# The opening of a two-layer encoder step: first loads reordered over two queues, first weights halved and scaled on ScalarE, spills held behind the first query weights

## The chip, the cores and the metric

The kernel runs on one core of a Trainium2 chip. The metric is the device time of one execution in microseconds (us), lower is better. Profiles are taken by the hardware profiler from one execution of the program. Engines are called PE (TensorE, matmul), DVE (VectorE), ACT (ScalarE), POOL (GpSimd) and SP (SyncE, which here only issues DMAs). PEld is the loading of PE's stationary operand, which runs beside its matmuls.

## The reference, cut to what matters

One inference step of a small encoder with two layers of width 1024. It takes a prompt of 1024 new frames and, beside it, 128 frames of eight running streams ("sample"). Both layers have attention and a squared-ReLU MLP; the first has its own queries, keys and values, the second shares one projection of keys and values. What the change touches is the opening of the first layer:

```
def rmsnorm(x, g):
    y = xf * lax.rsqrt(jnp.mean(xf * xf, axis=-1, keepdims=True) + EPS)
    return (y * g).astype(x.dtype)
...
def project_a(x, g_norm, w_qkv, g_q, g_k):
    qkv = rmsnorm(x, g_norm) @ w_qkv
    q, k, v = jnp.split(qkv, [1024, 1280], axis=-1)
    q = rmsnorm(q.reshape(b, t, 16, 64), g_q)
    k = rmsnorm(k.reshape(b, t, 4, 64), g_k)
    return q, k, v
```

After it come, for the prompt, attention over a window of whole chunks with a distance penalty and a learned sink, for the sample the same over a cache; then the output projection, the residual and the MLP. Everything is in float32.

## The kernel before, in words

**Precision.** A float32 operand is written as a sum of two parts, hi (rounded to the type that PE reads) and lo (the rest). A product takes three matmuls: hi by hi, hi by lo, lo by hi (`proj`, L178 to L184; in the profile L182, L183, L184 of a 128-row block k). So each operand of PE is first split, in two instructions: one rounds, one subtracts (`split`, L106 to L115, ACT and DVE as a rule).

**Tiles.** The 1024 prompt rows are eight tiles of 128 rows (t = 0 to 7), the 128 sample rows are a ninth, ST. The normalization is folded: the gain g goes into the rows of the weights, the row's inverse root mean square is applied later.

**Loads.** `load_block` (L122) brings a block of 1024 x 512 weights in four loads of two row blocks (512 KB), on SP's queue, into one of four raw buffers of [128, 2, 512]; `split_g` (L147) scales each row block k by its column of gains `gcol`: the hi part on POOL in this layer (L152; its configuration has the letter g), the lo part on DVE (L155). `prep_gains` (L1128) fills `gcol` before all else: five loads on SP (L1137), one transpose on PE in a PSUM pool of its own (L1139), one copy on DVE (L1140).

**The opening of layer 0** (L1514 on), with functions that are closures of `attention`:
- `X(t)` (L1304) loads a tile of x on SP's queue into one of two buffers "x" (L1313).
- `N(t)` (L1315) turns it: eight 128x128 transposes on PE (L175), two casts hh on ACT (L109) and two subtractions hl on DVE (L115); then the row statistics on ACT (L166) and small steps on DVE and POOL. Tile 0 has the buffers hh, hl (one of each), tile 1 borrows those of the attention's transposed probabilities, ST those of its probabilities p.
- `K1(t)` (L1365) is the projection of keys and values, eight row blocks of three matmuls with the block wkv; those of tiles 0, 1 and ST are woven, row block by row block (L1567). `K2(t)` (L1373) turns and splits the keys, and copies them half to half by two DMAs on SP (L278, L279).
- `Q1(t, 0)` (L1381) is the projection of the first half of the queries with the block wq, again eight row blocks of three; at its end ACT squares and copies the result (L191, L192; one buffer qr), DVE reduces, POOL takes the root (L203), DVE scales (L204). `Q2(t, 0)` (L1387) turns qr on PE (L225) and splits it into one of two buffers qT.
- `spill(t)` (L1339) stores hh and hl of a tile to device memory in four stores of 256 KB on SP (L1343), as the second half of the queries reads them back later (`R`, L1345).
- `sinks`, `load_gvec` load small constants on SP (L590, L1238 to L1247).

After the opening, a loop over steps and groups (`V`, `U`, plan) weaves scores, probabilities, transposes, later projections and the sample's units.

**What sets the order.** The code gives a program order, which is each instruction's priority. A scheduler then fixes the order of every engine's and queue's instructions by a simulated timeline: it picks, of what is ready in the simulation, the first by priority. Buffers of a pool are handed out in the same pass, and every wait is made from the resulting order. `behind(a, b)` (L715) adds an order between two instructions of a queue without a wait. In layer 0 no part has a raised priority, and no order is written out by hand.

Of the kernel before, what the change touches and what calls it, by code (L numbers as in the profile page):

```python
# [8 lines left out]
F32 = mybir.dt.float32  # L9
# [7 lines left out]
P = 128  # L17
D = 1024
KC = D // P
NT = 8  # L20
ST = NT
# [54 lines left out]
class Build:  # L76
# [44 lines left out]

    def load_block(self, dst, w, n0, g, ks=range(0, KC, 2)):  # L122
        nc = self.nc
        wr = w.rearrange("(k p) n -> p k n", p=P)
        for k0 in ks:
            raw = self.raw([P, 2, 512])
            nc.sync.dma_start(raw, wr[:, k0 : k0 + 2, n0 : n0 + 512])
            self.split_g(dst[:, 0, k0 : k0 + 2, :], dst[:, 1, k0 : k0 + 2, :], raw, g, k0)

# [16 lines left out]

    def split_g(self, hi, lo, raw, g, k0):  # L147
        nc = self.nc
        for k in range(raw.shape[1]):
            s = self.gcol[:, g * KC + k0 + k : g * KC + k0 + k + 1]  # L150
            if "g" in self.engs:
                nc.gpsimd.tensor_scalar(hi[:, k], raw[:, k], s, 1.0, ALU.mult, ALU.mult)  # L152
            else:
                nc.scalar.activation(hi[:, k], raw[:, k], AF.Copy, scale=s)
            nc.vector.scalar_tensor_tensor(  # L155
                lo[:, k], raw[:, k], s, hi[:, k].bitcast(F32), ALU.mult, ALU.subtract
            )
# [969 lines left out]

    def prep_gains(self):  # L1128
        nc, I = self.nc, self.ins
        with ExitStack() as st:  # L1130
            self.psum_pools(st, "pg", dict(m=(1, 1)), dict(m="m"))
            tmp = self.pool(st, "tmpg")
            g = tmp.tile([5 * KC, P], F32, tag="g", name="g")
            for i, v in enumerate(
                (I["g_attn"][0], I["g_attn"][1], I["g_mlp"][0], I["g_mlp"][1], I["g_kv"])
            ):
                nc.sync.dma_start(g[i * KC : (i + 1) * KC, :], v.rearrange("(k p) -> k p", p=P))  # L1137
            ps = self.psum("m", [P, 5 * KC], "ps_g")
            nc.tensor.transpose(ps, g, self.ident[0 : 5 * KC, 0 : 5 * KC])  # L1139
            nc.vector.tensor_copy(self.gcol, ps)  # L1140

# [10 lines left out]
    def run(self):  # L1152
# [9 lines left out]
        with ExitStack() as top:  # L1162
# [39 lines left out]

            self.prep_gains()
            flat = lambda a: a.rearrange("b s h d -> (b s) (h d)")
# [53 lines left out]
    def attention(self, layer):  # L1258
# [17 lines left out]
        with ExitStack() as st:  # L1276
# [27 lines left out]
            def X(t):  # L1304
                if A:
                    xr[t] = work.tile([P, D], F32, tag="x", name="x", bufs=2)
                elif t == ST:
                    nb = cfg["bias_bufs"]
                    x = ring.tile([P, G, 256], F32, tag="biasB", name="x", bufs=nb)
                    xr[t] = x.rearrange("p g k -> p (g k)")  # L1310
                else:
                    xr[t] = self.rawp.tile([P, D], F32, tag="raw", name="x")
# [26 lines left out]
            def spill(t):  # L1339
                for z in range(2):  # L1340
                    c = slice(4 * z, 4 * z + 4)
                    for v in range(2):
                        nc.sync.dma_start(self.hTd[t][:, v, c], hts[t][v][z].bitcast(F32))  # L1343

# [172 lines left out]
            wkv = self.wslot()  # L1517
            if A:
                X(0)
                self.load_block(wkv, wkv_src, kv0, gkv, [0])  # L1520
                X(1)
                N(0)
                self.load_block(wkv, wkv_src, kv0, gkv, [2])
                X(ST)
                N(1, "pt")
                self.load_block(wkv, wkv_src, kv0, gkv, [4, 6])
                N(ST, "p")
# [56 lines left out]
            spill(1)  # L1584
            run(Q1(1, 0, "s"))
            K2(1)
            spill(ST)
            run(Q1(ST, 0, "s"))
            K2(ST)
            X(2)  # L1590
            Q2(0, 0)
            N(2)
# [196 lines left out]
```

## Time and profile before

| | |
|---|---|
| median of 3 runs | 2400.1 us |
| lowest and highest | 2393.41 and 2401.02 us |
| the profiled execution's own time | 2396.21 us |
| its span, first to last instruction | 2394.4 us |
| mean granted clock of PE | 0.993 |
| bytes read and written in device memory | 246.47 and 136.14 MB |

The span lies 1.8 us inside the profiled execution's own time. A row of the order of time has the start and duration in us, the engine, the line, the operation, output and input by the program's names, and the count; in brackets the idle time of the engine before it and what ended it. SPq is SP issuing DMAs, not the transfer. A row of grouped instructions has the busy time and the mean ns of one. A row of stages gives the stretch, its length, and for each engine the busy time and count, then the clock that PE was granted (1.00 is full), the busy share of the 16 DMA engines and GB/s.

### The profile page before, as it was taken

The numbers are of one execution on the slowest core, as the hardware profiler recorded it, in microseconds if no ns is written. First come the engines' busy times: TensorE is split into PE (matmuls) and PEld (weight loads), VectorE is DVE, ScalarE is ACT, GpSimd is POOL, SyncE is SP. The second block draws the span as 40 slices with busy tenths as digits, with TensorE's granted clock in tenths as the row PEclk, the third lists the DMA queues.
The fourth block names the chain that finished last, engine by engine and source line by source line (L and its number), as shares of the span: only waits on it lengthen the run. The fifth ranks groups of instructions, "written<-read, shape, count | busy, mean of one in ns | idle before, by whom it ended". The sixth has DMA issues, their size and how long they took to land.

```text
span 2394.4 us, 33443 instructions
## 1 busy us (share of the span) xinstructions
PE 2315.4 (97%) x11621; PEld 1932.2 (81%) x11621; DVE 1629.9 (68%) x3002; ACT 1212.0 (51%) x2415; POOL 542.5 (23%) x836
## 2 busy tenths in 40 slices
PE   7999999899999999999999999998999999999999
PEld 6777877788888878888777788876888888888887
DVE  6787786755655767776577876877655555777674
ACT  3776675555555432332277666665555555323321
POOL 4343332312212100000243444444111211000000
PEclk9998999999999999999999999999999999999999
DMA  7345545344433874342754655555433445734332
GB/s 253 119 132 166 171 155 193 103 150 157 145 129 141 324 245 141 112 141 100 246 155 114 197 163 169 166 167 171 141 133 137 154 141 202 275 138 158 114 115 115
DMA packets 218393, 385.88 MB, mean 161 GB/s; under 512 B 50344, under 2 KB 125040, under 8 KB 211056
## 3 DMA queue, kind: packets, MB, share of 16 engines
q1 hardware_dynamic: 195152, 307.18, 39.0%
q0 software_dynamic: 21776, 71.84, 7.8%
q10 hardware_dynamic: 1296, 4.72, 0.5%
q8 instruction: 92, 1.51, 0.3%
q14 instruction: 77, 0.63, 0.1%
HBM read 246.47 MB, written 136.14 MB: 160 GB/s over the span
## 4 chain that ended last, share of the span: by engine, by line
PE 81%; DVE 7%; DMA 6%; ACT 3%; issue 2%; POOL 1%; SPq 0%; POOLq 0%; ACTq 0%; DVEq 0%
PE ps_x L711 9%; PE ps_x L713 9%; PE ps_x L712 9%; PE ps_y L713 7%; PE ps_y L712 7%; PE ps_y L711 7%; PE ps_mm L182 3%; PE ps_mm L184 3%; PE ps_mm L183 3%; PE ps_tr L289 2%; PE ps_mm L143 2%; PE ps_mm L145 2%; PE ps_mm L144 2%; PE ps_s L713 1%; PE ps_s L712 1%
## 5 line engine op out<-in xcount | busy, mean ns | idle before, releaser
L109 ACT CAST w<-r 128x2048 fp32r<-128x2048 f32 x56 | 107.1, 1913 | 321.6 <-PE ps_y L713 210.6
L711 PE MATMUL ps_x<-w,s 128*128 128x512 f32 x512 | 199.5, 390 | 4.3 <-DVE x L1017 2.2
L713 PE MATMUL ps_x<-w,s 128*128 128x512 f32 x512 | 199.4, 389 | 0.0
L712 PE MATMUL ps_x<-w,s 128*128 128x512 f32 x512 | 199.2, 389 | 0.0
L182 PE MATMUL ps_mm<-w,hh 128*128 128x512 f32 x432 | 174.2, 405 | 9.7 <-DMA hh<-hTd 3.3
L184 PE MATMUL ps_mm<-w,hl 128*128 128x512 f32 x432 | 174.1, 404 | 1.7 <-DMA hl<-hTd 1.6
L183 PE MATMUL ps_mm<-w,hh 128*128 128x512 f32 x432 | 172.5, 400 | 1.6 <-DVE w L155 1.6
L109 ACT CAST s<-s 128x2048 fp32r<-128x2048 f32 x56 | 107.2, 1914 | 121.3 <-DMA s<-hd 112.2
L115 DVE TENSOR_TENSOR w<-r,w 128x2048 fp32r<-128x2048 f32 x56 | 128.2, 2289 | 51.0 <-ACT w L109 51.0
L711 PE MATMUL ps_x<-sx,w 128*128 128x512 f32 (+1 forms) x408 | 157.9, 387 | 3.8 <-ACT hc L830 2.9
L1017 DVE TENSOR_TENSOR x<-ps_y,x 128x512 f32<-128x512 f32 x136 | 92.3, 687 | 99.8 <-PE ps_y L713 99.8
L713 PE MATMUL ps_x<-sx,w 128*128 128x512 f32 (+1 forms) x408 | 154.1, 378 | 0.0
L712 PE MATMUL ps_x<-sx,w 128*128 128x512 f32 (+1 forms) x408 | 154.1, 378 | 0.0
L109 ACT CAST w<-ru 128x512 fp32r<-128x512 f32 (+1 forms) x160 | 110.0, 708 | 85.4 <-PE ps_y L712 32.0
L713 PE MATMUL ps_y<-w,s 128*128 128x512 f32 x384 | 149.5, 389 | 0.0
L711 PE MATMUL ps_y<-w,s 128*128 128x512 f32 x384 | 149.4, 389 | 0.0
L712 PE MATMUL ps_y<-w,s 128*128 128x512 f32 x384 | 149.4, 389 | 0.0
L115 DVE TENSOR_TENSOR s<-s 128x2048 fp32r<-128x2048 f32 x56 | 128.0, 2286 | 30.4 <-ACT s L109 30.3
L115 DVE TENSOR_TENSOR ptl<-ps_tr,pth 128x512 fp32r<-128x512 f32 x180 | 122.6, 685 | 24.2 <-ACT pth L109 18.6
L115 DVE TENSOR_TENSOR w<-ru,w 128x512 fp32r<-128x512 f32 (+1 forms) x160 | 126.4, 792 | 11.2 <-ACT w L109 11.2
L115 DVE TENSOR_TENSOR wq<-ru,wq 128x1024 fp32r<-128x1024 f32 x32 | 39.7, 1240 | 132.2 <-ACT wq L109 132.2
L109 ACT CAST pth<-ps_tr 128x512 fp32r<-128x512 f32 x180 | 104.8, 595 | 45.6 <-PE ps_tr L289 33.2
(279 smaller groups left out, 6570.6 us busy)
## 6 DMA issues: line engine op xcount, KB each, us to landing
s<-hd SPq DMA_DIRECT2D x56, 1024.0 KB, 4.7
ru<-in_w_up SPq DMA_DIRECT2D x64, 512.0 KB, 3.8
r<-in_w_down SPq DMA_DIRECT2D x32, 1024.0 KB, 5.8
hd<-hc POOLq DMA_DIRECT2D x128, 256.0 KB, 2.7
hd<-hs POOLq DMA_DIRECT2D x96, 256.0 KB, 2.5
x<-xd SPq DMA_DIRECT2D x41, 512.0 KB, 4.5
o<-oTd SPq DMA_DIRECT2D x52, 256.0 KB, 3.9
hTd<-hh SPq DMA_DIRECT2D x36, 256.0 KB, 3.9
```

The source lines that it names most:

```text
L109: a = nc.scalar.copy(hi, src)
L115: return a, e.tensor_tensor(lo, src, hi.bitcast(F32), ALU.subtract)
L143: nc.tensor.matmul(ps, oh[:, k, :], w[:, 0, k, nn], start=(k == 0), stop=False)
L144: nc.tensor.matmul(ps, oh[:, k, :], w[:, 1, k, nn], start=False, stop=False)
L145: nc.tensor.matmul(ps, ol[:, k, :], w[:, 0, k, nn], start=False, stop=(k == 3))
L182: nc.tensor.matmul(ps, a, w[:, 0, k, :], start=(k == 0), stop=False)
L183: nc.tensor.matmul(ps, a, w[:, 1, k, :], start=False, stop=False)
L184: nc.tensor.matmul(ps, b, w[:, 0, k, :], start=False, stop=(k == KC - 1))
L711: a = mm(ps, ah, bh, start=first, stop=False, skip_group_check=True)
L712: mm(ps, ah, bl, start=False, stop=False, skip_group_check=True)
L713: return a, mm(ps, al, bh, start=False, stop=last, skip_group_check=True)
L1017: tt(xs[t][:, N[n]], ps, xs[t][:, N[n]], ALU.add)
```

## The change

It touches the opening of layer 0 in six ways.

1. The gains are loaded by `load_gains` on ACT's queue in three loads instead of five on SP's, into a buffer of the attention's pool, and turned by `turn_gains` in the attention's PSUM bank, after `N(0)`.
2. In program order the loads are x(0), the first two row blocks of wkv, x(1), the next two, x(ST), the last four. `N(0)` stands ahead of the first weights.
3. The wkv loads come in pieces of one row block (256 KB), and their hi part is scaled on ACT (`first=True`). Later blocks keep 512 KB and POOL.
4. x(ST) lies in one of the two qT buffers instead of one of the two x buffers.
5. Each weight load of `load_block` is kept as `self.gate`; the spills of tiles 0, 1 and ST are ordered on their queue behind the last of them, which is then the last piece of the first query weights wq.
6. `Q2(0, 0)` stands before `K2(1)` instead of after the load of x(2).

```diff
-    def load_block(self, dst, w, n0, g, ks=range(0, KC, 2)):
+    def load_block(self, dst, w, n0, g, ks=range(0, KC, 2), first=False):
...
             raw = self.raw([P, 2, 512])
-            nc.sync.dma_start(raw, wr[:, k0 : k0 + 2, n0 : n0 + 512])
-            self.split_g(dst[:, 0, k0 : k0 + 2, :], dst[:, 1, k0 : k0 + 2, :], raw, g, k0)
+            step = 1 if first else 2
+            for k in range(0, 2, step):
+                self.gate = nc.sync.dma_start(
+                    raw[:, k : k + step], wr[:, k0 + k : k0 + k + step, n0 : n0 + 512]
+                )
+            self.split_g(dst[:, 0, k0 : k0 + 2, :], dst[:, 1, k0 : k0 + 2, :], raw, g, k0, first)
...
-            if "g" in self.engs:
+            if "g" in self.engs and not first:
                 nc.gpsimd.tensor_scalar(hi[:, k], raw[:, k], s, 1.0, ALU.mult, ALU.mult)
             else:
                 nc.scalar.activation(hi[:, k], raw[:, k], AF.Copy, scale=s)
...
-    def prep_gains(self):
+    def load_gains(self, pool):
         nc, I = self.nc, self.ins
...
+        g = pool.tile([5 * KC, P], F32, tag="pvt", name="g", bufs=1)
+        n = 2 * KC
+        for i, v in enumerate((I["g_attn"], I["g_mlp"])):
+            nc.scalar.dma_start(g[i * n : (i + 1) * n, :], v.rearrange("l (k p) -> (l k) p", p=P))
+        nc.scalar.dma_start(g[2 * n :, :], I["g_kv"].rearrange("(k p) -> k p", p=P))
+        return g
+
+    def turn_gains(self, g):
+        nc = self.nc
+        ps = self.psum("m", [P, 5 * KC], "ps_g")
+        nc.tensor.transpose(ps, g, self.ident[0 : 5 * KC, 0 : 5 * KC])
+        nc.vector.tensor_copy(self.gcol, ps)
...
-            self.prep_gains()
...
-                if A:
+                if A and t == ST:
+                    xr[t] = apool.tile([P, D], F32, tag="qT", name="x", bufs=2)
+                elif A:
...
-                        nc.sync.dma_start(self.hTd[t][:, v, c], hts[t][v][z].bitcast(F32))
+                        d = nc.sync.dma_start(self.hTd[t][:, v, c], hts[t][v][z].bitcast(F32))
+                        if t in (0, 1, ST):
+                            self.behind(self.gate, d)
...
             if A:
+                g = self.load_gains(apool)
                 X(0)
-                self.load_block(wkv, wkv_src, kv0, gkv, [0])
+                N(0)
+                self.turn_gains(g)
+                self.load_block(wkv, wkv_src, kv0, gkv, [0], True)
                 X(1)
-                N(0)
-                self.load_block(wkv, wkv_src, kv0, gkv, [2])
+                self.load_block(wkv, wkv_src, kv0, gkv, [2], True)
                 X(ST)
                 N(1, "pt")
-                self.load_block(wkv, wkv_src, kv0, gkv, [4, 6])
+                self.load_block(wkv, wkv_src, kv0, gkv, [4, 6], True)
                 N(ST, "p")
...
             run(Q1(1, 0, "s"))
+            Q2(0, 0)
             K2(1)
             spill(ST)
             run(Q1(ST, 0, "s"))
             K2(ST)
             X(2)
-            Q2(0, 0)
             N(2)
```

More of the change, by code (lines that the diff above doesn't have):

```diff
@@ L145, in wo_proj, with split_g @@
             nc.tensor.matmul(ps, ol[:, k, :], w[:, 0, k, nn], start=False, stop=(k == 3))
-    def split_g(self, hi, lo, raw, g, k0):
+    def split_g(self, hi, lo, raw, g, k0, first=False):
         nc = self.nc
@@ L1126, in prep_bias @@
             nc.sync.dma_start(self.biasSd[0:KV].rearrange("j p c -> p j c"), big)
-    def prep_gains(self):
+    def load_gains(self, pool):
         nc, I = self.nc, self.ins
[L1130 to L1140, printed above, removed]
+        g = pool.tile([5 * KC, P], F32, tag="pvt", name="g", bufs=1)
[9 more added lines that the diff above has]
+        nc.vector.tensor_copy(self.gcol, ps)
     def token_scales(self, t, need_r):
```

## The prediction

> **What bounds the kernel now.** I read the page first (how busy TensorE, PE, is), then the busy time by stages, then the order of time of single engines where PE is not full.
>
> ```profile
> span 2394.4 us, 33443 instructions
> PE 2315.4 (97%) x11621; PEld 1932.2 (81%) x11621; DVE 1629.9 (68%) x3002; ACT 1212.0 (51%) x2415; POOL 542.5 (23%) x836
> ```
>
> PE is the bound: only 2394.4 - 2315.4 = 79 us of the span are without a matmul. The change can win idle PE time or PE time at a low clock, and only at the start. The stages (stretch, its length, busy us and count of PE, PEld, DVE, ACT, POOL; then granted clock, DMA share, GB/s):
>
> ```profile
> core 0: us, PE busy (x) PEld busy (x) DVE busy (x) ACT busy (x) POOL busy (x), PEclk, DMA share, GB/s
> 4.03:6.54 2.51, 0.30 (x1) 0.18 (x1) 0.20 (x1) 0.08 (x1) 0.00 (x0) 1.00 0.90 323
> 6.54:10.20 3.66, 3.63 (x16) 3.27 (x16) 1.67 (x6) 3.58 (x7) 0.60 (x2) 1.00 1.00 340
> 10.20:13.20 3.00, 0.02 (x1) 0.00 (x0) 2.64 (x5) 0.64 (x2) 3.00 (x5) 1.00 0.94 358
> 15.50:20.65 5.15, 5.14 (x12) 4.08 (x13) 5.11 (x11) 1.15 (x2) 2.71 (x3) 0.50 0.48 168
> 20.80:52.06 31.26, 31.26 (x146) 25.84 (x145) 18.64 (x37) 7.29 (x18) 14.89 (x18) 1.00 0.75 272
> 52.06:56.00 3.94, 2.14 (x19) 1.90 (x18) 3.01 (x7) 3.90 (x8) 2.15 (x2) 1.00 0.76 225
> 56.00:80.00 24.00, 21.48 (x104) 17.20 (x104) 17.34 (x65) 14.64 (x47) 6.75 (x13) 0.93 0.51 167
> ```
>
> PE in order of time (start, duration, and the idle time before it with its releaser):
>
> ```profile
> 4.06 0.30 PE L1139 MATMUL ps_g<-identr,g 40*128 40x40 f32 x1 [4.06 <-DMA g<-in_g_kv]
> 6.57 3.65 PE L175 MATMUL ps_n<-identr,x 128*128 128x128 f32 x16 [2.21 <-DMA x<-in_x_prompt]
> 13.20 0.73 PE L182 MATMUL ps_mm<-w,hh 128*128 128x512 f32 x2 [2.99 <-POOL w L152]
> 15.51 0.80 PE L183 MATMUL ps_mm<-w,hh 128*128 128x512 f32 x1 [1.57 <-DVE w L155]
> 23.65 1.03 PE L175 MATMUL ps_n<-identr,x 128*128 128x128 f32 x8
> ```
>
> The first projection matmul comes at 13.20, after PE has waited for x, then for weights scaled by POOL and DVE. At clock 0.50 twelve matmuls take 5.15 us, 0.43 each. From 20.80 PE is full for 31.26 us: 132 matmuls of 512 columns and 14 small ones (0.13 each by the 23.65 row), so (31.26 - 1.8)/132 = 0.22 each. All 144 matmuls of K1 and the first Q1 thus cost 32 us at full clock, whatever the loads do. The question is when PE reaches that steady stream. My **mark** is 20.80: 15 projection matmuls and 16 transposes done, clock about to be full.
>
> **The change, part by part.** First SP's queue:
>
> ```profile
> 0.74 0.38 SPq L1172 DMA_DIRECT2D eye<-in_eye  x1
> 1.18 0.69 SPq L1137 DMA_DIRECT2D g<-in_g_attn  x2
> 2.59 0.30 SPq L1137 DMA_DIRECT2D g<-in_g_kv  x1
> 2.93 0.83 SPq L1313 DMA_DIRECT2D x<-in_x_prompt  x2
> 3.81 2.14 SPq L127 DMA_DIRECT2D raw<-in_w_qkv_a  x4
> 10.15 0.33 SPq L1313 DMA_DIRECT2D x<-in_x_sample  x1
> 31.60 1.77 SPq L1343 DMA_DIRECT2D hTd<-hl  x2
> 42.94 0.71 SPq L278 DMA_DIRECT2D KT<-KT  x1
> ```
>
> *Gains.* Five issues leave SP; x(0) can go out at 1.18 instead of 2.93, 1.75 us sooner, and land near 4.8 instead of 6.54. Three issues of about 0.35 us come to ACT's queue, where nothing runs before 6.46 but the table load below; even behind it the gains land about 1.5 us after 3.1 (at 2.59 issued, at 4.06 used), so at 4.6. They are wanted at 7.3, so they cost nothing; 2.7 us of cover. Their 0.30 us transpose moves behind those of x(0).
>
> *Pieces and order.* In SP's queue stand x(0), then 256 KB of weights, and again, then x(1). At the 323 to 358 GB/s of the stages a 256 KB piece takes 0.75 us, so the first scaled row block lands near 5.6 and the second near 6.3, where the first 512 KB now land at 10.16. Four issues of some 0.4 us are added, in a queue whose engines are full, so nothing.
>
> The Trainium skill ("DMA: Bandwidth & Descriptors", section Bandwidth) advises transfers of at least 1 MiB and speaks against halving them; its formula of about 2.0 us plus bytes by 436 GB/s would make the estimate 2.6 us for a piece and 3.2 for the whole. The share of 0.90 to 1.00 here shows the engines full with 512 KB in flight beside others, so I do not charge it.
>
> *Scaling on ACT.* The rows for prices (busy, mean ns):
>
> ```profile
> 0.73 1.28 ACT L166 ACT_TABLE_LOAD   x1 [0.73 <-PEq L1771]
> 6.46 1.06 ACT L166 ACTIVATE junk<-x 128x1024 bf16<-128x1024 f32 x1 [4.44 <-DMA x<-in_x_prompt]
> L109 ACT CAST hh<-ps_n 128x512 fp32r<-128x512 f32 x8 | 4.4, 587 | 4.7 <-PE ps_n L175 4.6
> L109 ACT CAST w<-ru 128x512 fp32r<-128x512 f32 x128 | 76.4, 621 | 48.5 <-DVE ru L774 23.6 <-DVE ru L771 22.1 <-DVE ru L773 2.8
> L155 DVE SCALAR_TENSOR_TENSOR w<-raw,gcol,w x16: 737/1171/1178, 10.9 to 34.9; 128x512 fp32r<-128x512 f32 x16
> L115 DVE TENSOR_TENSOR hl<-ps_n,hh 128x512 fp32r<-128x512 f32 x8 | 5.3, 684 | 0.5 <-ACT hh L109 0.3
> 10.16 1.36 POOL L152 TENSOR_SCALAR w<-raw,gcol 128x512 fp32r<-128x512 f32 x2 [1.72 <-DMA raw<-in_w_qkv_a]
> 33.07 1.36 POOL L152 TENSOR_SCALAR w<-raw,gcol 128x512 fp32r<-128x512 f32 x2 [2.02 <-DMA raw<-in_w_qkv_a]
> ```
>
> The eight scalings of wkv leave POOL (0.68 each) for ACT. The trace has no scaled 128x512 from SBUF on ACT; its bounds are 0.59 (hh cast) and 0.70, and I take the 0.62 of the row with the same operands. DVE's half (L155) takes 0.74 where POOL is silent and 1.17 beside POOL, by its minimum and median: with POOL out it should be 0.74. ACT then has three statistics (1.06 + 0.19), six casts of 0.59 and eight scalings: 3.75 + 3.5 + 5.0 = 12.3 us from 4.8, to 17.1 if never idle. DVE has 8 x 0.74 + 6 x 0.69 = 10.1 us from 6.7, with 0.9 of small work to 17.7.
>
> *The first matmul.* x(0) lands at 4.8; eight transposes at 0.228 (3.65/16) end at 6.7; ACT does the statistics 4.8 to 6.05, the casts to 7.3, the first scaling to 7.9: PE starts near 8.1, 5.1 us sooner. From there 15 matmuls plus the 8 transposes each of x(1) and the sample tile stand before the new mark, the latter a 1.03 us which now comes after 20.80. If all is at half clock: 16 x 0.228 + 15 x 0.43 = 10.1, the mark at 18.1, and the gain 20.8 + 1.03 - 18.1 = 3.7. If the clock is full after 4 us of it (8 transposes in 1.8, 5 matmuls in 2.2), the rest is 1.03 + 10 x 0.22 = 3.2, the mark at 15.3 and the gain 6.5. The present clock filled about 5.2 us after its steady stream began (15.50 to 20.65), so I take full clock after 6.4 us: 1.8 + 11 x 0.43 = 6.5, then 1.03 + 4 x 0.22 = 1.9, the mark at 16.5, **gain 5.4**, between 3.7 and 6.5. ACT and DVE end the weights at 17 to 18; PE wants nine matmuls a row block (2 us), so it is not starved after the mark.
>
> *The sample tile* gets its own buffer: its load no longer waits for x(0)'s (10.15) and lands with the weights; counted in the mark.
>
> *Spills behind wq.* Twelve stores of 256 KB (3.1 MB, 9 us at 350 GB/s) now stand among the wq pieces, up to 31.60; POOL scales the last wq piece from 33.07 on, when it has landed. Behind the gate wq's 2.1 MB follow wkv's and the x tiles' 3.7 MB: 5.8 MB at 350 GB/s from 3.3 on (of the 3.6 us from issue to use of x(0), 1.5 are its bytes) end at 20, with waits for raw buffers (free as DVE ends, 17.7) an estimated 20 to 22. PE does not wait for wq now (31.26 busy of 31.26), so this wins nothing itself; it keeps PE fed in the earlier start. Queued behind on SP are the copies of KT (42.94), near 36 in the new time; stores from 21 on end near 30. Cover 6 us; if it is gone, the first scores wait as long as the copies are late.
>
> *Q2(0,0) before K2(1).* The rows:
>
> ```profile
> 44.43 0.94 DVE L204 TENSOR_TENSOR qr<-qr,qrs 128x512 f32<-128x512 f32 x1 [0.71 <-POOL qrs L203]
> 53.89 0.58 ACT L192 COPY qr<-ps_mm 128x512 f32<-128x512 f32 x1
> 54.84 0.59 ACT L109 CAST hh<-ps_n 128x512 fp32r<-128x512 f32 x1
> 54.59 0.69 DVE L204 TENSOR_TENSOR qr<-qr,qrs 128x512 f32<-128x512 f32 x1
> 55.34 0.66 PE L225 MATMUL ps_q<-identr,qr 128*128 128x128 f32 x4 [1.80 <-DVE qr L204]
> 100.00:120.00 20.00, 20.00 (x118) 17.06 (x117) 16.66 (x55) 15.45 (x44) 8.17 (x15) 1.00 0.37 116
> 176.12 0.33 PE L570 MATMUL ps_utp<-identr,sp 128*128 128x128 f32 x1 [3.24 <-DVE w L155]
> 180.71 0.77 PE L182 MATMUL ps_mm<-w,hh 128*128 128x512 f32 x1 [3.14 <-DMA hh<-hTd]
> 172.60:181.00 8.40, 2.02 (x12) 1.36 (x11) 8.24 (x19) 5.67 (x12) 1.71 (x2) 0.82 0.84 280
> ```
>
> The one qr buffer is ready at 45.37, but its transposes come only at 52.06 and the next copy into it at 53.89; PE then waits 1.80 us. Early transposes (0.6 us of PE, the same work) free the buffer by 47; that stall goes, and late next is the hh of tile 2, cast at 54.84. Between 0 and 3 us; I take **1.5**.
>
> **Sum.** 5.4 + 1.5 = 6.9 us. PE is full from 100 to 120 (the stage row above), so a shift before should pass on. The profiled execution took 2396.2 and the median of the runs is 2400.1; from their middle, 2398.2, comes 2391.3. A measurement of this kernel tells some 0.3%, 7.2 us, from no change.
>
> **The rivals.** *More goes with it* (0.22). From 56 to 80 PE idles 2.5 us and loses 1.7 us to a clock of 0.93; with 1.1 us to the mark's upper bound that is 5.3 more: 2386. For: it is the same qr chain. Against: other waits stand there.
>
> *The clock stays low* (0.20). ACT hands over weights in pieces, PE has gaps, and the half clock lasts to 18: 3.7 + 0 = 3.7, hence 2394.5. For: the gaps of 2.99 and 1.57 us above preceded 0.50. The Trainium skill ("TensorE: Matmul & The Clock Gate", Part 1) says that the clock opens after about 3.4 us of sustained work and (Part 4) that transposes do not count as such; by that rule an earlier, thinner stream buys nothing at full rate. The trace agrees in that 16 transposes before did not spare the 0.50.
>
> *Slower* (0.10). The order in the attention stage comes from a simulated timeline, so a new start can reorder it. The place is the pair of stalls at 172 to 181, 3.24 + 3.14 us with 8.4 x 0.18 = 1.5 us of low clock: 7.9. Two more such pairs give 2391.3 + 15.8 = 2407; from 14.1 us of added stalls on it is slower by over 0.3%. Against: the order is local, the later work unchanged.
>
> *Not what it says* (0.03). The code before has weights ahead of x(1), yet SP issues both x first; if the scheduler turns the new order back, 2398.
>
> **How the numbers follow.** The forecast has 0.45, of which 0.33 lie below 2392.9 (faster) and 0.12 above. Faster 0.33 + 0.22 = 0.55; same 0.12 + 0.20 + 0.03 = 0.35; slower 0.10. The range 2382 to 2400 takes in the bounds (6.5 + 3 and the 5 us more; 3.7 with nothing) and leaves out the slower case and tails.
>
> **What would show it.** Right: x(0) transposes at 5, first L182 near 8, L155 at 0.74 for wkv, the mark near 16.5, spills after the last wq piece, Q2(0) before 47, PE at 100 us some 7 us ahead. Wrong: ACT idle on DMA with casts behind it, clock 0.50 past 18, KT copies late, or new PE waits beyond 100 us.

## The result, and the profile after

The changed kernel takes 2401.24 us (median of 22 runs, 2391.75 to 2409.3), the kernel before in the same comparison 2395.18 us (22 runs, 2389.15 to 2402.3). The ratio is 1.0022 with a 95% interval of 1.0011 to 1.0032: it is **slower**, by about 5.3 us, where 2391.3 and a gain were forecast. The profiled execution took 2401.08 us. All line numbers of the changed kernel's opening have moved: L182 to L184 are L186 to L188, L155 is L159, L225 is L229, L242 is L246, L1343 is L1349.

The page of the changed kernel:

```profile
span 2399.3 us, 33421 instructions
PE 2320.4 (97%) x11621; PEld 1935.5 (81%) x11621; DVE 1626.3 (68%) x3002; ACT 1217.9 (51%) x2423; POOL 535.6 (22%) x828
```

The span is 4.9 us longer, and PE's busy time 5.0 longer, with the same 11621 matmuls. So the page says nothing of where the loss is: idle PE time is 79 us as before, since a matmul's modelled length (0.39 us where two starts lie 0.23 apart) hides gaps shorter than itself, and matmuls at half clock count as busy. I therefore counted the projection matmuls (rows of PE with output ps_mm) in the order of time, and noted when the n-th of them starts. Four profiles have layer 0 as in the kernel before, so they show how far this varies without a change:

| start of the n-th in layer 0, us | 72 | 96 | 216 | 312 |
|---|---|---|---|---|
| layer 0 as before, four profiles | 33.7 to 34.8 | 39.1 to 40.2 | 80.8 to 83.3 | 121.5 to 124.0 |
| changed kernel | 28.1 | 39.2 | 80.7 | 126.3 |

A lead of 6 us stands at the 72nd matmul, is gone at the 96th, and has become a loss at the 312th. First the start. PE of the changed kernel in the order of time:

```profile
5.85 1.94 PE L179 MATMUL ps_n<-identr,x 128*128 128x128 f32 x8 [5.85 <-DMA x<-in_x_prompt]
8.70 1.97 PE L179 MATMUL ps_n<-identr,x 128*128 128x128 f32 x8 [0.66 <-DMA x<-in_x_prompt]
10.32 0.78 PE L186 MATMUL ps_mm<-w,hh 128*128 128x512 f32 x1
11.32 0.57 PE L188 MATMUL ps_mm<-w,hl 128*128 128x512 f32 x1
11.72 0.39 PE L186 MATMUL ps_mm<-w,hh 128*128 128x512 f32 x1
32.48 0.77 PE L186 MATMUL ps_mm<-w,hh 128*128 128x512 f32 x1 [4.01 <-ACT kw L253]
54.63 0.63 PE L229 MATMUL ps_q<-identr,qr 128*128 128x128 f32 x4 [1.94 <-DVE qT L115]
```

x(0) comes at 5.85, the first projection matmul at 10.32, and the matmuls are 0.23 apart from 11.72 on: the start works. But at 28.5 us, with K1 of three tiles (72 matmuls) done, PE stands still for 4.01 us, and the matmuls behind that are at half clock again (0.77 and more). The releaser is ACT's kw, the reading of K1(0)'s PSUM bank, which Q1(0) needs. What that reading waits for is on VectorE of the changed kernel:

```profile
22.36 4.04 DVE L159 SCALAR_TENSOR_TENSOR w<-raw,gcol,w 128x512 fp32r<-128x512 f32 x4 [1.91 <-POOL w L156]
29.46 1.83 DVE L159 SCALAR_TENSOR_TENSOR w<-raw,gcol,w 128x512 fp32r<-128x512 f32 x2 [3.06 <-POOL w L156]
31.21 0.47 DVE L246 SCALAR_TENSOR_TENSOR VS<-ps_mm,rx,VS 128x256 fp32r<-128x256 f32 x1
```

L246 takes the values out of K1(0)'s bank. In DVE's queue it stands behind the scalings of the first query weights (L159 at 29.46), and these wait for POOL, which waits for transfers. So late query weights hold up PE through the queue of another engine, before PE wants the weights themselves. They are late only beside PE: POOL starts on the last of them at 31.29 us, which is 1.8 us sooner than before (33.07), while PE comes some 6 us sooner. Why they gain so little is on SP's queue of the changed kernel:

```profile
11.95 2.30 SPq L1251 DMA_DIRECT2D ssink<-in_sink_a  x4
14.37 1.05 SPq L129 DMA_DIRECT2D raw<-in_w_qkv_a  x2
15.82 1.84 SPq L1319 DMA_DIRECT2D x<-in_x_prompt  x2
19.23 0.52 SPq L129 DMA_DIRECT2D raw<-in_w_qkv_a  x1
21.60 0.37 SPq L129 DMA_DIRECT2D raw<-in_w_qkv_a  x1
22.90 0.34 SPq L1349 DMA_DIRECT2D hTd<-hh  x1
```

The spills do stand behind the last piece (22.90). But the sinks still stand ahead of all four pieces, as they did before, and x(2), x(3) and the first caches, which before went out at 24.2 to 28.7 us around the last piece, now stand ahead of the third.

The third place is at 90 to 127 us. The stages of the changed kernel there:

```profile
90.00:95.00 5.00, 2.81 (x22) 2.29 (x21) 3.69 (x16) 4.83 (x11) 3.97 (x7) 1.00 0.01 2
105.00:110.00 5.00, 3.93 (x26) 2.85 (x25) 4.61 (x16) 4.72 (x14) 1.84 (x4) 1.00 0.22 54
110.00:115.00 5.00, 4.54 (x23) 3.42 (x23) 3.53 (x8) 2.00 (x5) 1.24 (x2) 1.00 0.28 86
```

PE, which before was busy for 4.90 of the 5 us from 90 to 95 and full from 100 to 120, now idles 2.2, 1.1 and 0.5 us. Its waits there, in the order of time:

```profile
93.99 0.50 PE L300 MATMUL ps_pv<-pth,VS 128*128 128x512 f32 x1 [1.92 <-ACT pth L109]
108.19 0.50 PE L349 MATMUL ps_s<-KT,qT 128*128 128x256 f32 x2 [0.57 <-DVE qT L115]
```

The fourth place is one that the prediction never looked at, the opening of **layer 1** in the changed kernel:

```profile
1189.42 0.50 PE L186 MATMUL ps_mm<-w,hh 128*128 128x512 f32 x1 [0.98 <-POOL w L156]
1190.63 0.50 PE L187 MATMUL ps_mm<-w,hh 128*128 128x512 f32 x1 [0.71 <-DVE w L159]
```

The kernel before has no such waits. The hold of the spills and the place of Q2(0,0) lie in code that both layers run, so both edits change layer 1 too, though the section on the change speaks of layer 0 alone.

### The profile page after: what moved, and what is told of

It is laid out like the page before. It is cut to its first block, busy times and chain, and to the rows that moved or that the text cites. A ratio compares the mean times of both kernels' runs of the same rounds, so it can differ in the third digit from the quotient of the medians.

```text
span 2399.3 us, 33421 instructions
## 1 busy us (share of the span) xinstructions
PE 2320.4 (97%) x11621; PEld 1935.5 (81%) x11621; DVE 1626.3 (68%) x3002; ACT 1217.9 (51%) x2423; POOL 535.6 (22%) x828
## 4 chain that ended last, share of the span: by engine, by line
PE 82%; DMA 7%; DVE 5%; ACT 2%; issue 2%; POOL 1%; SPq 1%; ACTq 0%; DVEq 0%; POOLq 0%
PE ps_x L715 9%; PE ps_x L717 9%; PE ps_x L716 9%; PE ps_y L717 7%; PE ps_y L716 7%; PE ps_y L715 7%; PE ps_mm L186 3%; PE ps_mm L188 3%; PE ps_mm L187 3%; PE ps_tr L293 2%; PE ps_mm L147 2%; PE ps_mm L149 2%; PE ps_mm L148 2%; PE ps_s L717 1%; PE ps_s L716 1%
## 5 line engine op out<-in xcount | busy, mean ns | idle before, releaser
L186 PE MATMUL ps_mm<-w,hh 128*128 128x512 f32 x432 | 175.0, 407 | 13.8 <-ACT kw L253 5.1
L188 PE MATMUL ps_mm<-w,hl 128*128 128x512 f32 x432 | 174.3, 403 | 1.7 <-DMA hl<-hTd 1.4
```

The lines of the kernel that those rows point to most:

```text
L186: nc.tensor.matmul(ps, a, w[:, 0, k, :], start=(k == 0), stop=False)
L188: nc.tensor.matmul(ps, b, w[:, 0, k, :], start=False, stop=(k == KC - 1))
```

## The experiments

The kernels were measured in four comparisons, each with its own runs of the kernel before: e1 to e4; e9 to e12; e13 with e5 to e7; e14, e16 and e8. They are told here by what they tell apart. The openings are read as above; in layer 1, from its first projection matmul on. Where neither edit touches layer 1 (eleven profiles, the kernel before among them), the 100th starts 23.6 to 24.6 us and the 216th 62.6 to 65.1 us after the first.

**First: which layer, and which part.** The two edits were taken out of layer 1; put alone into layer 1 of the kernel before; and each undone in both layers.

```diff
 e1_layer0_only (of the changed kernel)
-                        if t in (0, 1, ST):
+                        if A and t in (0, 1, ST):
...
-            Q2(0, 0)
+            if A:
+                Q2(0, 0)
...
+            if not A:
+                Q2(0, 0)
 e2_layer1_only (of the kernel before): the same two edits with "not A"
 e3_no_gate (of the changed kernel)
-                        if t in (0, 1, ST):
-                            self.behind(self.gate, d)
 e4_q2_back (of the changed kernel): Q2(0, 0) after X(2) again
```

> The changed kernel with its two parts that also reach layer 1 (the order of the spills behind the weights, and the place of Q2(0,0)) kept to layer 0; layer 1's code is that of before. Theory L1 (the loss is made in layer 1's opening by these two parts, which the prediction did not look at): it gains over the changed kernel what that lost there, about 4 us, and stands at 0.9985 to 1.0005 of before. Rival L0 (the loss is layer 0's: PE starves for the last query weights near 30 us and goes to half clock): like the changed kernel, 1.001 to 1.003 of before. Rival R (the new start reorders all of the program, and the loss is spread over it): also 1.001 to 1.003, with the lag growing outside both openings.

> The kernel before with only the two parts in layer 1: spills of tiles 0, 1 and ST ordered behind the last query weights, and Q2(0,0) ahead of K2(1); layer 0 as before. L1: slower by 3 to 6 us, 1.0015 to 1.0025 of before. L0 and R: no difference, 0.9995 to 1.0005.

> The changed kernel without the order of the spills behind the weights, in both layers. L1: gains the larger share of 4 us over the changed kernel, as the spills of layer 1 go out again in the idle DMA time before the last query weights. L0: the spills again go among the query weights, so PE starves as long or longer near 30 us; no gain or a loss of 1 to 3 us there. R: unforeseeable within 4 us either way.

> The changed kernel with Q2(0,0) back at its old place in both layers. The prediction's step: slower by 0 to 3 us than the changed kernel. L1 by way of Q2: faster by up to 2 us, as K2(1) and its copies of KT go out sooner in layer 1 (1194.4 and 1203.9 in the changed kernel, 1191.3 and 1198.8 before). R: within 4 us either way.

| kernel | ratio to before | 95% interval |
|---|---|---|
| e1_layer0_only | 1.0015 | 1.0005 to 1.0025 |
| e2_layer1_only | 1.0034 | 1.0021 to 1.0046 |
| e3_no_gate | 1.0030 | 1.0017 to 1.0042 |
| e4_q2_back | 1.0004 | 0.9992 to 1.0016 |

None of the three theories holds alone. e2 shows layer 1's part, against L0 and R: with layer 0 as before, it is as slow as the changed kernel or slower, more even than L1 expected. But e1 shows, against L1, that layer 0's part by itself is no gain either. Taking Q2 back (e4) wins most of the loss, some 4 us where at most 2 were expected. Taking the hold away (e3) doesn't, and in its layer 0 PE's wait before the 73rd matmul is 3.78 us, nearly that of the changed kernel: that wait comes with the new start, held spills or not.

**Second: each of the two edits alone, in one layer, on the kernel before.**

> The kernel before with the spills of tiles 0, 1 and ST held behind the first query weights in layer 1 alone, nothing else. If the hold costs layer 1 what the openings show (3 us between the first and the 100th projection matmul), 1.001 to 1.002; the distance from the first to the 100th is 26.5 to 27.5 us against 23.7. If layer 1's loss comes from the early Q2 only, 1.000 and 23.7.

> The kernel before with Q2(0,0) put ahead of K2(1) in layer 1 alone. From the run of both parts there (1.0034) and the openings (2.8 us from the first to the 216th projection matmul): 1.001 to 1.002, with the first to the 100th unchanged at 23.7 and the first to the 216th at 67 against 64. If the early Q2 costs nothing by itself and only the hold does: 1.000.

> The kernel before with Q2(0,0) put ahead of K2(1) in layer 0 alone. The prediction had it gain 0 to 3 us. From the runs with and without it in layer 0 (1.0015 against 0.9986, the new loads and the hold in both): it loses 4 to 7 us, 1.0015 to 1.003. If it only lets the new order of loads gain less (because it stands in the same place where TensorE waits for the query weights), it is 0.999 to 1.0005 here, where the loads are the old ones.

> The kernel before with the spills of tiles 0, 1 and ST held behind the first query weights in layer 0 alone; TensorE's order is that of the kernel before, instruction by instruction. The prediction priced this part at nothing. If that holds: 0.9995 to 1.0005, openings alike (the 100th projection matmul at 40 to 41.5 us). If the hold gives the query weights the transfers earlier, the 100th comes 1 to 2 us earlier and the time is 0.9992 to 0.9997; if the spills come late for tile 0's reload or for the KT copies, 1.001.

| kernel | ratio to before | 95% interval | us |
|---|---|---|---|
| e7: Q2 early, layer 0 | 1.0017 | 1.0007 to 1.0027 | +4.1 |
| e6: Q2 early, layer 1 | 1.0012 | 1.0001 to 1.0022 | +2.9 |
| e5: hold, layer 1 | 1.0006 | 0.9997 to 1.0015 | +1.4 |
| e8: hold, layer 0 | 1.0005 | 0.9994 to 1.0016 | +1.2 |

The early Q2 costs in both layers, as expected. In e7 the openings agree with the kernel before up to the 240th matmul (90.3 us), and the 312th comes at 127.1 instead of 121.5 to 124.0: 36.8 us for these 72 against 32.5. This is the place at 90 to 127 us of the changed kernel, with the same first wait. PE of e7:

```profile
94.71 0.49 PE L296 MATMUL ps_pv<-pth,VS 128*128 128x512 f32 x1 [1.61 <-ACT pth L109]
```

All four kernels with the early Q2 in layer 0 need 36.6 to 37.0 us there; those without need 32.4 to 32.5 whatever else they change. The scheduler, given Q2 earlier, orders PE's work otherwise far past the edit (in e7 at 48 places, 43 of them among the first 2000 of its 11621 matmuls), and in that order PE reaches a product of probabilities before ACT has cast them.

For the hold the times alone leave open whether it costs at all: both intervals take in 1, and e5 is under the 1.001 expected. The openings show where it costs; that of e8 is none of the three expected. In e8 PE's order is that of the kernel before, instruction by instruction, and the 96th matmul comes at 42.6 instead of 39.1 to 40.2 (PE of e8):

```profile
37.25 0.47 PE L182 MATMUL ps_mm<-w,hh 128*128 128x512 f32 x1 [2.51 <-ACT kw L249]
```

That is the wait of the changed kernel at 32 us, with the old loads. VectorE's queue tells why, in the kernel before and then in e8:

```profile
30.42 1.17 DVE L155 SCALAR_TENSOR_TENSOR w<-raw,gcol,w 128x512 fp32r<-128x512 f32 x1 [1.11 <-POOL w L152]
31.51 0.47 DVE L242 SCALAR_TENSOR_TENSOR VS<-ps_mm,rx,VS 128x256 fp32r<-128x256 f32 x1
```

```profile
26.93 1.83 DVE L155 SCALAR_TENSOR_TENSOR w<-raw,gcol,w 128x512 fp32r<-128x512 f32 x2 [3.45 <-POOL w L152]
30.50 5.56 DVE L155 SCALAR_TENSOR_TENSOR w<-raw,gcol,w 128x512 fp32r<-128x512 f32 x5 [0.54 <-POOL w L152]
35.99 0.47 DVE L242 SCALAR_TENSOR_TENSOR VS<-ps_mm,rx,VS 128x256 fp32r<-128x256 f32 x1
```

Before, the eviction stands behind five scalings of the query weights; with the spills held back it stands behind seven (six in the changed kernel). The order is fixed by a simulated timeline, and VectorE keeps it, though POOL delivers the first of these weights no sooner than before (26.20 us in e8, 24.18 in the kernel before), since x(2) and the first caches go out ahead of them.

In layer 1 the hold brings the weights no sooner either. SP's queue in the kernel before and in e5:

```profile
1181.23 1.37 SPq L127 DMA_DIRECT2D raw<-in_w_q_b  x2
```

```profile
1175.84 2.03 SPq L127 DMA_DIRECT2D raw<-in_w_q_b  x2
1177.91 0.46 SPq L1343 DMA_DIRECT2D hTd<-hh  x1
```

The first projection matmul is at 1165.9 there and at 1160.9 here, so the last two pieces go out 15.3 and 14.9 us behind it, at nearly the same place: the spills did not hold them up. The spills went out meanwhile; now all twelve follow. Ten microseconds of both, from 9 us behind the first projection matmul, before and then e5:

```profile
1175.00:1185.00 10.00, 10.00 (x45) 8.29 (x45) 6.53 (x13) 1.85 (x5) 4.18 (x5) 1.00 1.06 381
```

```profile
1170.00:1180.00 10.00, 10.00 (x46) 8.27 (x45) 6.52 (x13) 2.59 (x7) 4.99 (x6) 1.00 0.71 231
```

And PE's order has changed: twelve Q1 matmuls stand ahead of the first keys' transposes, and want weights that aren't there. PE of e5:

```profile
1184.34 0.50 PE L182 MATMUL ps_mm<-w,hh 128*128 128x512 f32 x1 [1.06 <-POOL w L152]
1185.55 0.50 PE L183 MATMUL ps_mm<-w,hh 128*128 128x512 f32 x1 [0.71 <-DVE w L155]
```

The 100th comes 27.6 us after the first here (23.7 before), and 26.4 to 28.0 in all four kernels with the hold in layer 1. In e6, with the early Q2 alone, the 100th is where it was (23.8) and the 216th comes 66.4 us after the first; with both edits in layer 1 it is 68.8 and 70.8.

**Third: the new start without these costs, and what holds it up.** e9 has the new start, the hold in layer 0 alone and Q2 at its old place. The other three change the order of transfers in it; PE's order of instructions is the same in all four.

```diff
 e9_start_only (of the changed kernel): Q2(0, 0) after X(2) again, and
-                        if t in (0, 1, ST):
+                        if A and t in (0, 1, ST):
 e10_hold (of e9)
-                nc.sync.dma_start(xr[t], x_src(t))
+                d = nc.sync.dma_start(xr[t], x_src(t))
+                if A and t in (2, 3):
+                    self.behind(self.gate, d)
... (g_mlp likewise)
 e11_sinks (of e9): sinks(ring) after the load of wq[0], and in it
-            nc.sync.dma_start(
+            d = nc.sync.dma_start(
                 self.ssink[i * 32 : i * 32 + 32, :],
...
+            self.behind(self.gate, d)
 e12_both: the edits of e10 and e11
```

> The changed kernel with Q2(0,0) at its old place in both layers and the spills held back in layer 0 alone, so that layer 1's opening is the old one and layer 0 keeps the new order of loads. If the loss of the changed kernel sits in layer 1's opening (the hold and the early Q2, some 3 us each there), this stands some 3 us under the run that only put Q2 back, which was 1.0004 of the kernel before: 0.9985 to 0.9995. If the start of layer 0 is really worth the 7 us that it shows at the 72nd projection matmul, it is 0.997. If it is the new order of TensorE's work through both attention layers (135 places differ from the kernel before) that costs, it is 1.001 or more, since that order stays.

> The run above with the loads of x for tiles 2 and 3 and of g_mlp in layer 0 ordered behind the last piece of the first query weights; TensorE's order is the same instruction by instruction. If layer 0's lead of 7 us is lost because those loads (1 MB of x and 0.5 MB of g_mlp) stand ahead of the last two weight pieces, the wait of TensorE at 28 to 32.5 us shrinks to 1 us or less, the 100th projection matmul comes near 37 us instead of 40, and the time is 3 us under the run above (ratio 0.9987 of it). If the loads of x are what then comes late, tile 2's transposes wait and the gain is taken back within the opening: same as the run above. If the hole in the transfers at 16 to 18 us sets the pieces' arrival, not their order, it gains under 1 us.

> The run before the last with the loads of the attention sinks (one of 128x16 and four of 32x4, whose elements of 4 bytes are gathered one by one) issued behind the last piece of the first query weights; TensorE's order is the same. If these loads make the hole in the transfers at 16 to 18 us (0 GB/s), it is gone or moves behind the weights, the last piece lands some 2 to 3 us earlier, and the time falls 1 to 3 us. If the hole comes from something else, the rate at 15 to 20 us stays near 80 GB/s and the time is the same.

> Both of the last two. If both the order and the hole hold the weights back, the last of the first query weights is in SBUF by 22 to 24 us, TensorE doesn't wait after the 15th projection matmul, the 100th comes near 36 us, and the time is 5 to 6 us under the first run of this call, about 0.997 of the kernel before. If the lead is lost elsewhere, the opening is shorter by this and the time is not.

| kernel | ratio to before | 95% interval | 72nd | 96th | wait of PE after the 72nd |
|---|---|---|---|---|---|
| e9_start_only | 0.9986 | 0.9976 to 0.9996 | 28.6 | 40.1 | 4.24 |
| e10_hold | 0.9999 | 0.9987 to 1.0011 | 29.2 | 40.9 | 4.39 |
| e11_sinks | 0.9989 | 0.9978 to 1.0001 | 28.0 | 38.7 | 3.46 |
| e12_both | 0.9982 | 0.9968 to 0.9996 | 28.2 | 38.9 | 3.40 |

e9 is faster than the kernel before by 3.4 us, although PE's order differs from it at 39 places, counted as in e7 (34 of them among the first 2000 matmuls; its expectation says 135). So a changed order does not cost by itself, and the start is worth something. Together the parts account for the change: -3.4 (e9, with its hold in layer 0) + 4.1 + 2.9 + 1.4 = 5.0 us, against 5.3 measured. (The four kernels of the first group lie 3 to 5 us above the sums of their parts, e2 for one at 8.1 against 4.3. The intervals of two to three us on each term don't settle that; all four are set against the same runs of the kernel before, so an error in those would shift them together. That the sum comes so near 5.3 may be luck in part.) The hold in layer 1 may cost more than e5's 1.4: e4 and e9 differ in it alone, and their ratios lie 0.0018 or 4.3 us apart, if in two comparisons.

e10 gains nothing, where 3 us were expected. Yet its trace shows that the order did hold the weights up: the last piece lands at 27.0 us instead of 31.7, and POOL no longer waits for it. The last scalings on POOL in e9, then in e10 with the eviction:

```profile
31.80 1.48 POOL L156 TENSOR_SCALAR w<-raw,gcol 128x512 fp32r<-128x512 f32 x2 [0.95 <-DMA raw<-in_w_qkv_a]
```

```profile
29.77 1.79 POOL L156 TENSOR_SCALAR w<-raw,gcol 128x512 fp32r<-128x512 f32 x2
32.69 0.86 DVE L246 SCALAR_TENSOR_TENSOR VS<-ps_mm,rx,VS 128x256 fp32r<-128x256 f32 x2
```

POOL is at the scalings until 31.6 us all the same, with 2.4 us of work on the cache between them, and the eviction now stands behind all eight scalings instead of six. So weights that land in time do not help as long as POOL and VectorE's order hold the eviction back.

e11 finds a second hold-up of the weights, the sinks' loads. The stages of e9 and then of e11:

```profile
16.00:17.00 1.00, 1.00 (x6) 0.84 (x5) 1.00 (x4) 0.88 (x2) 0.00 (x0) 1.00 0.04 0
17.00:18.00 1.00, 1.00 (x6) 0.81 (x6) 1.00 (x5) 0.00 (x0) 0.00 (x0) 1.00 0.03 0
```

```profile
16.00:17.00 1.00, 1.00 (x6) 0.84 (x5) 0.12 (x2) 1.00 (x2) 0.00 (x0) 1.00 1.01 403
17.00:18.00 1.00, 1.00 (x6) 0.81 (x5) 1.00 (x5) 0.09 (x1) 0.00 (x0) 1.00 1.06 429
```

With the sinks' loads behind the weights, transfers run at 403 and 429 GB/s where they stood at 0, and the last piece lands at 27.4 us. Yet PE's wait only shrinks from 4.24 to 3.46 us, and the time, of which 1 to 3 us were expected, doesn't tell e11 from e9. In e12 the last piece lands at 24.4 us, the wait is 3.40 us, and the time comes to 0.9982, not to the 0.997 expected. VectorE of e12 shows what is late next:

```profile
29.29 0.16 DVE L1261 TENSOR_TENSOR susink<-ssink,rsl 128x4 f32<-128x4 f32 x1 [1.78 <-DMA ssink<-in_sink_a]
29.39 1.42 DVE L159 SCALAR_TENSOR_TENSOR w<-raw,gcol,w 128x512 fp32r<-128x512 f32 x2
30.72 0.87 DVE L246 SCALAR_TENSOR_TENSOR VS<-ps_mm,rx,VS 128x256 fp32r<-128x256 f32 x2
```

The eviction L246 still stands behind the last scalings, which were paced by POOL until 28.0 us and then by a small operation that waits for the sinks just moved back.

**Fourth: the same chain, link by link.** ACT is idle from 17 to 27 us in e12, so it takes POOL's scalings of wq[0]: e13 on e12, e14 on e9 (which is the "first run" that its expectation names). e16 adds to e13 that DVE's two operations on the sinks stand behind L246. PE's and SP's order in e13 and e16 are those of e12.

```diff
 e13_act_wq (of e12), e14_act_alone (of e9)
-            self.split_g(..., raw, g, k0, first)
+            self.split_g(..., raw, g, k0, first or act)
...
-                self.load_block(wq[0], wq_src, 0, gq)
+                self.load_block(wq[0], wq_src, 0, gq, act=A)
 e16_sinks_late (of e13): usink and susink are computed after K1, with
+        self.behind(self.evict, a)
...
+        self.behind(self.evict, b)
```

> The last run of the call before (order of loads and sinks mended) with the first query weights of layer 0 scaled on ScalarE, which stands idle from 17 to 27 us, instead of GpSimd; the order of TensorE and of SP's transfers is the same, row for row. Theory: with the transfers mended TensorE still waited 3.4 us, because VectorE's eviction of the first K and V (L246) stands in its queue behind the eight scalings of the query weights (L159), which waited for GpSimd's; with ScalarE's 0.7 us each they are done near 26 us, the eviction follows K1's end at once, the wait at 28 to 32 us goes below 1 us, the half clock behind it goes too, the 100th projection matmul comes near 35.5 us instead of 40.0, and the time is 4 to 5 us under that run (0.9963 to 0.998 of the kernel before). Rival: the wait is for something else (the PSUM bank by ScalarE's copies, or the sinks that VectorE waits for until 29.3 us), TensorE goes on near 31.5 us as before, and the time is that of the last run (0.9982).

> The first run of the second call (the new start and the hold in layer 0 alone, Q2 at its old place; loads and sinks where the change has them) with the first query weights scaled on ScalarE instead of GpSimd. If GpSimd's scaling alone holds up the eviction, TensorE's wait of 4.2 us near 29 to 33 us falls under 2 us here. If the transfers hold it up as well (the last two pieces landed at 28 and 31 us in the changed kernel, behind a hole of 2 us and the loads of x), ScalarE scales them only then, the wait stays at 3 us or more, the 100th projection matmul stays near 40 to 41, and the time that of the run without it: 0.998 to 0.9995.

> The run with both the transfers mended and ScalarE scaling, with VectorE's two operations on the sinks put behind the eviction of the first K and V; TensorE's and SP's order unchanged. In that run VectorE stood 3.4 us idle for the sinks' landing at 29.6 us, with the last scaling and the eviction queued behind. Expected: the 1.0 us wait of TensorE at 31 us is gone, the first to the 216th projection matmul takes 1 us less (66.6 against 67.6 there, 70.1 in the kernel before), and the time is the lowest of the study: 0.9965 to 0.998. Rival: the lead is kept through layer 0's attention and lost further on, where TensorE waits for transfers that come at their own time; then the opening is shorter and the time stays near 0.9985.

| kernel | ratio to before | 95% interval | 72nd | 96th | 216th |
|---|---|---|---|---|---|
| e14_act_alone | 1.0022 | 1.0010 to 1.0033 | 28.9 | 40.8 | 85.5 |
| e13_act_wq | 0.9985 | 0.9973 to 0.9996 | 30.2 | 36.9 | 78.6 |
| e16_sinks_late | 0.9970 | 0.9959 to 0.9981 | 27.9 | 34.1 | 77.4 |

In e14 the scaling alone does nothing for the wait (4.67 us): VectorE there gets the last piece at 31.36, as its transfer landed at 30.6.

```profile
31.36 1.42 DVE L159 SCALAR_TENSOR_TENSOR w<-raw,gcol,w 128x512 fp32r<-128x512 f32 x2 [1.86 <-ACT w L158]
```

That was expected; its time was not. It loses 3.2 us more between the 96th and the 216th than e9; the scheduler has put its PE work in another order (36 places). The rest of its loss was not traced.

In e13 the wait falls to 1.03 us, about as the theory had it, and the 216th comes 1.9 us sooner than in e12 though the start of this profile was slow (x(1)'s transposes at 9.37, the clock full only at 15.5, 72nd at 30.2). Its time did not show it: 0.9985, just above the range expected. PE of e13, then VectorE:

```profile
31.59 0.50 PE L186 MATMUL ps_mm<-w,hh 128*128 128x512 f32 x1 [1.03 <-ACT kw L253]
```

```profile
29.62 0.17 DVE L1261 TENSOR_TENSOR susink<-ssink,rsl 128x4 f32<-128x4 f32 x1 [3.42 <-DMA ssink<-in_sink_a]
```

VectorE stands 3.42 us before that operation with the eviction behind it. e16 takes it out. VectorE of e16, then PE:

```profile
25.72 1.41 DVE L159 SCALAR_TENSOR_TENSOR w<-raw,gcol,w 128x512 fp32r<-128x512 f32 x2 [1.25 <-ACT w L158]
27.52 0.48 DVE L246 SCALAR_TENSOR_TENSOR VS<-ps_mm,rx,VS 128x256 fp32r<-128x256 f32 x1 [0.39 <-ACT VS L245]
```

```profile
28.77 0.50 PE L186 MATMUL ps_mm<-w,hh 128*128 128x512 f32 x1 [0.49 <-DVE usink L1257]
```

The wait is 0.49 us, the 96th comes at 34.1, 5 to 6 us ahead of the kernel before, and a lead of 3.4 to 5.9 stands at the 312th (118.1). At 2388.13 us, beside 2395.88 for the kernel before in the same comparison, e16 is the fastest kernel of the study, and its interval is clear of the kernel before and of the changed kernel: its ratio of 0.997, within what was expected, is 7.2 us. From the first to the 216th it takes 67.3 us, not the 66.6 expected. So with nearly the whole wait out the lead reaches the end. What each step is worth in time is not settled: the intervals of e9, e12, e13 and e16 overlap.

## Why the prediction was wrong

**The start: right.** The mark (read as the prediction read 20.80, the start of the 15th projection matmul) came at 15.2 us instead of 16.5. With the sample tile's transposes before it the gain by the prediction's own account is 20.8 + 1.03 - 15.2 = 6.6, against 5.4 and its upper bound of 6.5. Part of that is luck: the mark lies at 14.8 to 17.3 us in the ten other profiles with this start, and at 19.8 to 20.8 in the six with the old one. The pieces of it erred both ways: x(0) came at 5.85 instead of 4.8, ACT's scaling took 0.67 to 0.73 us instead of 0.62, the first matmul started at 10.32 instead of 8.1 (x(1)'s transposes stand ahead of it), and the clock was full at 11.72, behind three projection matmuls instead of eleven. VectorE's 0.74 beside a silent POOL held. One reading of the trace was wrong: "16 transposes before did not spare the 0.50". They had opened the clock, and the idle stretch behind them lost it (last section).

**The step that failed first** is that of the spills: "Behind the gate wq's 2.1 MB follow wkv's and the x tiles' 3.7 MB ... with waits for raw buffers ... an estimated 20 to 22", which "keeps PE fed in the earlier start". The last piece landed near 31 us, its last scaling ended on VectorE at 34.2, and PE stood 4.01 us. The bytes were counted, but not the stretch at 0 GB/s that the sinks' loads make (the kernel before has one too, 1 GB/s from 18 to 19 us), nor the two x tiles that go ahead of the third piece, nor POOL's pace. The hold does not feed PE: without it (e3) the wait is 3.78 us. And the wait came by a way that was not looked for: not PE wanting wq, but the eviction of K1's bank in VectorE's queue behind wq's scalings. "PE does not wait for wq now (31.26 busy of 31.26)" was true because PE was later and the eviction stood elsewhere in the queue, not because the weights had slack. e8 shows the order; e10 to e12 show that earlier weights alone leave 3.4 us or more of the wait, e14 that faster scalings alone leave 4.67, e13 that both together leave 1.03, and e16 that 0.49 is left with the sinks out of VectorE's way.

**The second** is "Early transposes ... free the buffer by 47; that stall goes ... Between 0 and 3 us; I take 1.5". Q2(0,0) ran at 48.77 us instead of 52.06, but a stall of 1.94, now for qT, stands where that of 1.80 for qr stood, and the edit costs 4.1 us in layer 0 (e7), at 90 to 127 us. That is the mechanism of the rival *Slower*, an order from the simulated timeline that brings PE to its inputs too early. It had a chance of 0.10, a place (172 to 181) that was wrong, and a price of 15.8 us that was too high.

**The third** is no number but a scope: the sum has terms for layer 0 only. The same lines run in layer 1, where the early Q2 costs 2.9 us (e6) and the hold 1.4 by time, 4 by the opening (e5). The hold, of which the prediction says "this wins nothing itself", has no cost in the sum; that was wrong in layer 1 and, by the opening of e8, in layer 0.

**PE at 100 us "some 7 us ahead"** was the test that would have told: it was level at the 96th matmul, at 39 us, already.

## What to carry to other kernels

Before pricing an earlier start, ask of every stream behind it (weights, evictions, queue order) whether it has slack or was just in time, and follow each engine's queue, since a wait may sit in front of an unrelated instruction. Look for all places where an edited line runs: a second layer has other waits, and one order that costs 3 us there can eat a gain here. Where a scheduler lays out the order, an edit of one line is an edit of everything behind it, so test its parts one by one and compare when the n-th matmul starts, not busy shares.

## What the runs showed of the hardware

- **Four loads of 512 bytes each, of elements of 4 bytes, stop the queue.** Of the sinks' four loads in e9 the three whose landing the profile tells took 5.7 to 8.2 us from issue to landing, and the large transfers issued behind them moved at 0 GB/s for 2 us. Moved back, the hole moved with them: in e12, with the spills behind them, 1 and 0 GB/s from 24 to 26 us. VectorE operations that need them waited until 20 us in the changed kernel and 29 us in e12. Whether it is the small elements, the repetition over partitions or the single load of 128x16 beside them that is slow was not tried.
- **Transposes open the clock here, and an idle stretch loses it.** In the kernel before, PE had run only transposes when the clock was granted in full; it was at half by 14.2 us, behind the idle stretch of 2.99 us. Two stages of it:

```profile
10.80:14.10 3.30, 0.73 (x2) 0.30 (x2) 3.21 (x4) 0.04 (x1) 3.30 (x6) 1.00 0.77 286
14.20:20.95 6.75, 5.44 (x13) 4.28 (x14) 6.41 (x13) 1.15 (x2) 4.01 (x4) 0.50 0.51 179
```

A stage row shows 1.00 also where the profile has no record of the clock yet (as that from 6.54 to 10.20 does), so the pace has to confirm it. The first two projection matmuls took 0.73 us together here (the row at 13.20 in the prediction) but 1.22 in e5, where the clock was not open. PE of e5:

```profile
12.76 1.22 PE L182 MATMUL ps_mm<-w,hh 128*128 128x512 f32 x2 [2.32 <-POOL w L152]
```

In e6 and e7, too, the clock opened during the transposes: the last two start 0.15 us apart in e6 and 0.11 in e7, those before 0.21. In e2, e5 and e8, with the same start, it did not. In the changed kernel, with 0.66 us idle between the transposes, the matmuls are at full rate (0.23 us apart) from 11.72 us, 5.9 us after the first transpose, with only three projection matmuls before; in the eleven profiles with the new start the clock is full from 11.3 to 15.5 us. The Trainium skill ("TensorE: Matmul & The Clock Gate", Part 4) says that transposes do not count as PE-busy for the clock; by that rule sixteen transposes or three matmuls of some 0.5 us would not have opened it. These traces do not agree.
- **A wait of 4 us costs more than itself.** After it the matmuls at 32.48 us and on ran 0.43 us apart for 3 us before the clock was full again, some 1.5 us more. The waits of 2.51 us in e8, 1.03 in e13 and 0.49 in e16 at this place left the clock at 1.00.
